# A one-pass score product for the row maximum, and the exact scores turned by keys, in the attention of a two-layer encoder trunk

## The chip, the cores and the metric

The kernel runs on one core of a Trainium2 chip. The metric is the device time of one execution in microseconds (us). A core has a matrix engine (PE, TensorE, with its weight loads shown apart as PEld), a vector engine (DVE), an activation engine (ACT), a general engine (POOL, GpSimd) and a queue engine (SP) that here only issues transfers. Each works through its own instructions in the order in which they stand; an instruction waits until the ones it depends on, on other engines, are done, and whatever stands behind it on the same engine waits with it.

## The reference, cut to what matters

Two layers work on 512 tokens of width 1024. A layer has a first gated feed-forward step, a mixing step and a second feed-forward step, with norms between. The mixing step has two groups side by side: attention with 8 heads, and a causal convolution over the tokens with 31 taps on 512 channels, followed by a layer norm over the channels and a swish. Both are put side by side and go through one output product.

```
scores = einsum('bhqd,bhkd->bhqk', qs, ks) * scale          # per block of 128 queries, keys up to the block's end
scores = where(k_chunk <= q_chunk, scores, -1e30)           # chunks of 64 tokens
probs  = softmax(scores)
out    = einsum('bhqk,bhkd->bqhd', probs, vs)
...
y = conv(u, conv_w) + conv_b                                # 31 taps, each channel for itself
conv = silu(layer_norm(y))
x = x + concat(attn, conv) @ w_out
```

So a head needs, for every query, the exponential of its scores less something near the largest of them, the sum of these, and the product with the values.

## The kernel before

All products of activations and weights run as three one-pass products of rounded parts (`mm3`, lines 151 to 154: high by high, high by low, low by high; the rounded type is called fp32r). Inside the attention the products are of the full four-byte type f32.

The mixing step of a layer is one function, `mix_body`. It makes the latents, queries and keys, then works through the heads in a software pipeline (lines 874 to 880): the string `ORDER` (line 58) gives each stage a lag in heads, so that step s works on head s in `turn`, head s-1 in `scores`, head s-3 in `turn_p`, and so on.

- `turn` (L804, L809) transposes a head's queries and keys on PE, 4 blocks each, so that the 100 rows (96 features and 4 rows that carry the chunk mask) lie on partitions. ACT writes the queries with their gain (L806), DVE the keys (L811).
- `scores` (L824) takes for each of the four blocks of 128 queries the product with the 128, 256, 384 or 512 keys that it may see; DVE finds the negated maximum of each row (L825), ACT takes the exponential with it as bias (L829). Queries lie on partitions.
- `turn_p` (L843) transposes the 10 blocks of probabilities on PE, and DVE, ACT and DVE copy them back (L846).
- `values` (L854) takes the 10 products of turned probabilities with 65 columns, 64 of values and one of ones, which gives the sum; DVE divides (L860, L861).
- `turn_out` (L871) transposes each pair of heads, and the result is cut into a high and a low part.

The convolution stands behind the heads in the program but has other operands. `CONV = "DAAD"` (line 42) says who does it: chunks 0 and 3 on DVE (L894), chunks 1 and 2 by ACT, which scales a shifted copy (L898, into one of three buffers called `pr`), and POOL, which adds it up (L902), 30 taps to a chunk. I call "tap n" the addition with n columns; the second chunk on POOL (the tile y_2856 in layer 0, y_2859 after the change) runs from tap 511 down to tap 482. POOL then adds the four chunks (L916 to L918), and PE takes the mean over channels with a matrix of 1/512 (L920, into `pm`). Behind L920 stand, on PE, the first half of the output product for three groups (`early_groups`, L909 to L912, which needs only the attention), then the rest of the layer norm and of the output product.

What sets the order: the program is given to a scheduler that plays it through with its own durations and fixes the order of the instructions on each engine. What it fixed is not changed while the kernel runs. Two lines hold it: the taps from the sixteenth of chunk 1 on, and all of chunk 2, must stand behind the last rsqrt of the keys (L901), and the early groups behind the last head's exponential (L909).

Of the kernel before, what the change touches and what calls it, by code (L numbers as in the profile page):

```python
# [15 lines left out]
P = 128  # L16
D = 1024
S = 512
# [6 lines left out]
DQ = DN + DR  # L25
DM = DQ + 4
DV = 64
# [18 lines left out]
POOLW = "wo"  # L46
QFOLD = 0
EARLY = "s"
# [7 lines left out]
WOP = 4  # L56
EVP = "DAD"
ORDER = "t0s1p3v4o5"

# [13 lines left out]
def encoder_kernel(ctx: ExitStack, tc: tile.TileContext, xT, consts, vecs, rgain, wgu1, wd1,  # L73
# [23 lines left out]
    def bank():  # L97
        return psum.tile([P, S], FP, tag="ps", name=nm("ps"))
# [26 lines left out]
    V.memset(onesm, 1.0 / CW)  # L125
    marks = cpool.tile([P, 2, NT, NT], FP, name="marks")
    G.memset(marks, 0.0)
    for t in range(NT):
        G.memset(marks[0:64, 0, t, t:t + 1], 1.0)
        G.memset(marks[64:P, 1, t, t:t + 1], -1e30)  # L130
# [478 lines left out]
    def mix_body(kpool, l, gx, norm, done):  # L609
# [3 lines left out]
        def glu(pa, pg):  # L613
# [7 lines left out]
            u.append(uc)  # L621

        def conv_in(c):
            pp = []
            for j in range(2):
                ps = bank()
                group(ps, load_w(wcv[l, 2 * c + j], WC, f"c{c}"), gx, range(KD), KD)
                pp.append(ps)
            glu(*pp)

# [11 lines left out]
        for side, v in enumerate((q, kn)):  # L642
            G.tensor_copy(v[:, :, :, DQ:DM], marks[:, side, :, None, :].to_broadcast([P, NT, H, NT]))
        cq, wkl_, sk, ckc, ratio = (tiny(n, NT) for n in ("cq", "wkl", "sk", "ckc", "ratio"))
# [80 lines left out]
        def queries():  # L725
            wq = [load_w(wuq[l, :, k * 768:(k + 1) * 768], 768, "uq") for k in range(3)]
            for t in range(NT):
# [17 lines left out]
                if t % 2:  # L745
                    rope(q[:, t - 1:t + 1, :, DN:DQ], tabs[0][:, :, t - 1:t + 1], H)
                    if not QFOLD:
                        for i in (t - 1, t):
                            V.tensor_tensor(q[:, i, :, 0:DQ], q[:, i, :, 0:DQ], scqs[i][:, :, None].to_broadcast([P, H, DQ]),
                                            ALU.mult)  # L750

# [49 lines left out]
        def turn(h):  # L801
            ps = bank()
            for t in range(NT):
                T.transpose(ps[0:DM, t * P:(t + 1) * P], q[:, t, h], ident)  # L804
            qT = slot()
            A.activation(qT[0:DM], ps[0:DM], AF.Copy, scale=gqs[0:DM])  # L806
            ps = bank()
            for t in range(NT):
                T.transpose(ps[0:DM, t * P:(t + 1) * P], kn[:, t, h], ident)  # L809
            kT = slot()  # L810
            V.tensor_scalar(kT[0:DM], ps[0:DM], gk, None, ALU.mult)  # L811
            heads[h]["qk"] = qT, kT

        def scores(h):
            qT, kT = heads[h]["qk"]
            b01, b2, b3 = bank(), bank(), bank()
            mx = small.tile([P, NT], FP, tag="mx", name=nm("mx"), bufs=3)
            pi = []
            ps = [slot() for _ in range(3)]
            ps = [ps[0][:, 0:128], ps[0][:, 128:384], ps[1][:, 0:384], ps[2]]  # L820
            for i in range(NT):
                n = (i + 1) * P
                o = (b01[:, 0:128], b01[:, 128:384], b2[:, 0:384], b3)[i]
                heads[h]["s"] = T.matmul(o, qT[0:DM, i * P:(i + 1) * P], kT[0:DM, 0:n], start=True, stop=True).ins  # L824
                V.tensor_reduce(mx[:, i:i + 1], o, axis=AX.X, op=ALU.max, negate=True)  # L825
                p = ps[i]
                if QFOLD:
                    V.tensor_tensor(mx[:, i:i + 1], mx[:, i:i + 1], scqs[i][:, h:h + 1], ALU.mult)
                A.activation(p, o, AF.Exp, bias=mx[:, i:i + 1], scale=scqs[i][:, h:h + 1] if QFOLD else 1.0)  # L829
                pi.append(p)  # L830
            heads[h]["p"] = pi

        def turn_p(h):

            pi = heads[h]["p"]
            pt = []
            for js, eng in (((0,), EVP[0]), ((1, 3), EVP[1]), ((2,), EVP[2])):
                ps = bank()
                sb = slot()
                o = 0  # L840
                for j in js:
                    for i in range(j, NT):
                        heads[h]["t"] = T.transpose(ps[:, o:o + P], pi[i][:, j * P:(j + 1) * P], ident).ins  # L843
                        o += P
                    pt.append((j, sb[:, o - (NT - j) * P:o]))
                (A.copy if eng == "A" else V.tensor_copy)(sb[:, 0:o], ps[:, 0:o])  # L846
            heads[h]["pt"] = [p for _, p in sorted(pt, key=lambda e: e[0])]

# [24 lines left out]

        STAGES = [({"t": turn, "s": scores, "p": turn_p, "v": values, "o": turn_out}[c], int(d)) for c, d in zip(ORDER[::2], ORDER[1::2])]
# [287 lines left out]
```

## Time and profile before

| | us |
|---|---|
| median of 3 runs | 1766.07 (1764.32 to 1767.33) |
| the profiled execution's own time | 1766.88 |
| its span, first to last instruction | 1765.1 |
| PE busy | 1745.7 (99%) |
| DVE, ACT, POOL busy | 1400.8, 942.5, 271.4 |
| start of the heads' scores on PE, layer 0 and 1 | 448.37, 1321.84 |
| start of L920, layer 0 and 1 | 503.06, 1376.49 |

The page gives a busy time per engine over the whole span; the stage that the change is in is about 70 us of each layer. There the timeline (start, duration, engine, line, shape, count, and in brackets the idle time before with what ended it) and the windows (busy time of each engine in a stretch, with counts) are what is to be read. A row of the timeline merges neighbours: "x26" is 26 instructions, and its duration runs from the start of the first to the end of the last. An f32 product with 128 to 512 columns makes two records on PE, a transpose makes one. Durations of single PE products overlap their neighbours, so what a product costs is read from start to start.

### The profile page before, as it was taken

The numbers are of one execution on the slowest core, as the hardware profiler recorded it, in microseconds if no ns is written. First come the engines' busy times: TensorE is split into PE (matmuls) and PEld (weight loads), VectorE is DVE, ScalarE is ACT, GpSimd is POOL, SyncE is SP. The second block draws the span as 40 slices with busy tenths as digits, with TensorE's granted clock in tenths as the row PEclk, the third lists the DMA queues.
The fourth block names the chain that finished last, engine by engine and source line by source line (L and its number), as shares of the span: only waits on it lengthen the run. The fifth ranks groups of instructions, "written<-read, shape, count | busy, mean of one in ns | idle before, by whom it ended". The sixth has DMA issues, their size and how long they took to land.

```text
span 1765.1 us, 22117 instructions
## 1 busy us (share of the span) xinstructions
PE 1745.7 (99%) x8102; PEld 1448.1 (82%) x8102; DVE 1400.8 (79%) x2033; ACT 942.5 (53%) x1420; POOL 271.4 (15%) x234
## 2 busy tenths in 40 slices
PE   9999999999999999999999999999999999999998
PEld 7888888888788888888888888888887888888886
DVE  8967878679869877869799778866889698678884
ACT  7544445457955544445555344444679455344453
POOL 2000000048942000000000000000579400000000
PEclk9999999999999999999999999999999999999999
DMA  9354434424225355352924445343251444544345
GB/s 294 129 179 138 139 119 122 141 76 123 60 108 132 129 158 167 96 167 83 293 89 142 145 132 167 95 144 107 79 137 31 147 106 136 174 143 145 106 134 153
DMA packets 121917, 236.70 MB, mean 134 GB/s; under 512 B 10705, under 2 KB 58321, under 8 KB 121809
## 3 DMA queue, kind: packets, MB, share of 16 engines
q1 hardware_dynamic: 117488, 222.08, 39.3%
q0 software_dynamic: 3456, 12.58, 3.9%
q8 instruction: 63, 1.03, 0.2%
q10 hardware_dynamic: 864, 0.64, 0.1%
q14 instruction: 46, 0.37, 0.1%
HBM read 207.99 MB, written 25.17 MB: 132 GB/s over the span
## 4 chain that ended last, share of the span: by engine, by line
PE 83%; DMA 6%; DVE 4%; ACT 2%; POOL 2%; issue 2%; SPq 1%; POOLq 0%; ACTq 0%; DVEq 0%
PE ps L154 26%; PE ps L152 26%; PE ps L153 26%; PE ps L854 2%; DMA fr<-in_wgu 2%; POOL y L902 1%; DVE wl L239 1%; DMA raw<-in_wgu 1%; PE ps L824 1%; DMA d<-e 1%; DMA r<-d 1%; PE ps L843 1%; ACT pr L898 1%; DVE fr L336 0%; ACT r L829 0%
## 5 line engine op out<-in xcount | busy, mean ns | idle before, releaser
L153 PE MATMUL ps<-wl,r 128*128 128x512 f32 (+2 forms) x1434 | 548.5, 384 | 1.4 <-DVE wl L239 1.4
L154 PE MATMUL ps<-wh,r 128*128 128x512 f32 (+2 forms) x1434 | 545.6, 384 | 0.2 <-DVE r L265 0.2
L152 PE MATMUL ps<-wh,r 128*128 128x512 f32 (+2 forms) x1434 | 530.2, 385 | 2.2 <-ACT wh L237 1.7
L237 ACT CAST wh<-fr 128x1024 fp32r<-128x1024 f32 x255 | 267.1, 1049 | 237.6 <-PE ps L153 108.6
L154 PE MATMUL ps<-r,wl 128*128 128x512 f32 x944 | 366.3, 390 | 0.7 <-POOL wl L147 0.5
L153 PE MATMUL ps<-r,wh 128*128 128x512 f32 x944 | 366.2, 390 | 0.0
L152 PE MATMUL ps<-r,wh 128*128 128x512 f32 x944 | 362.4, 393 | 1.1 <-ACT r L394 0.3
L239 DVE TENSOR_TENSOR wl<-fr,wh 128x1024 fp32r<-128x1024 f32 x255 | 310.1, 1219 | 52.0 <-ACT wh L237 51.0
L152 PEld LDWEIGHTS ps<-wh,r 128*128 128x128 f32 x1434 | 270.1, 189 | 55.2 <-ACT wh L237 2.6
L153 PEld LDWEIGHTS ps<-wl,r 128*128 128x128 f32 x1434 | 269.9, 188 | 53.9 <-DVE wl L239 1.9
L154 PEld LDWEIGHTS ps<-wh,r 128*128 128x128 f32 x1434 | 269.8, 188 | 52.4 <-DVE r L265 0.6
L141 ACT CAST wh<-raw 128x1024 fp32r<-128x1024 f32 (+2 forms) x142 | 139.7, 989 | 216.4 <-PE ps L153 96.5
L152 PEld LDWEIGHTS ps<-r,wh 128*128 128x128 f32 x944 | 177.1, 188 | 41.2 <-ACT r L394 1.7
L154 PEld LDWEIGHTS ps<-r,wl 128*128 128x128 f32 x944 | 177.2, 188 | 38.9 <-POOL wl L147 1.3
L153 PEld LDWEIGHTS ps<-r,wh 128*128 128x128 f32 x944 | 177.3, 188 | 38.4 <-issue 1.4
L147 DVE TENSOR_TENSOR wl<-raw,wh 128x1024 fp32r<-128x1024 f32 (+3 forms) x126 | 145.9, 1159 | 76.4 <-ACT wh L141 75.6
L902 POOL TENSOR_TENSOR y<-y,pr 128x511 f32<-128x511 f32 (+14 forms) x120 | 158.4, 1320 | 51.1 <-ACT pr L898 43.6
L336 DVE TENSOR_TENSOR fr<-fr,fr 128x1024 f32<-128x1024 f32 x112 | 136.6, 1220 | 12.6 <-DMA fr<-in_wgu 12.6
L484 DVE TENSOR_TENSOR x<-ps,x 128x512 f32<-128x512 f32 x120 | 81.5, 686 | 54.4 <-PE ps L154 54.1
L366 ACT ACTIVATE e<-e,rtok 128x256 f32<-128x256 f32 x120 | 59.9, 507 | 79.1 <-DVE e L357 78.4
L898 ACT ACTIVATE pr<-r,vec 128x511 f32<-128x511 f32 (+14 forms) x120 | 85.0, 734 | 13.7 <-POOL y L902 13.7
L395 DVE TENSOR_TENSOR r<-r,r 128x512 fp32r<-128x512 f32 x88 | 58.0, 681 | 41.5 <-ACT r L394 41.4
(197 smaller groups left out, 1668.2 us busy)
## 6 DMA issues: line engine op xcount, KB each, us to landing
fr<-in_wgu SPq DMA_DIRECT2D x175, 512.0 KB, 4.2
raw<-in_wd SPq DMA_DIRECT2D x56, 512.0 KB, 4.3
d<-e SPq DMA_DIRECT2D x176, 128.0 KB, 3.1
r<-d SPq DMA_DIRECT2D x88, 256.0 KB, 3.2
raw<-in_wd SPq DMA_DIRECT2D x32, 384.0 KB, 3.9
raw<-in_wcv SPq DMA_DIRECT2D x16, 512.0 KB, 3.3
raw<-in_wout SPq DMA_DIRECT2D x16, 512.0 KB, 4.1
raw<-in_wgu SPq DMA_DIRECT2D x8, 512.0 KB, 8.8
```

The lines of the kernel that those rows point to most:

```text
L141: A.copy(hi[:, :w], raw[:, :w])
L147: (G if kind in POOLW.split() else V).tensor_tensor(lo[:, :w], raw[:, :w], hi[:, :w].bitcast(FP), ALU.subtract)
L152: T.matmul(o, lh, rh, start=first, stop=False, skip_group_check=free)
L153: T.matmul(o, lh, rl, start=False, stop=False, skip_group_check=free)
L154: T.matmul(o, ll, rh, start=False, stop=last, skip_group_check=free)
L237: order["cast"] = A.copy(hi[:, :w], src[:, :w]).ins
L239: V.tensor_tensor(lo[:, :w], src[:, :w], hi[:, :w].bitcast(FP), ALU.subtract)
L336: V.tensor_tensor(oh, ah, bh, ALU.add)
L366: A.activation(out[j][:, :h], src[j][:, :h], AF.Silu, scale=r)
L484: V.tensor_tensor(xm, pd.rearrange("p (a t j) -> p t a j", a=4, t=NT), xm, ALU.add)
L898: A.activation(pr[:, s:], u[c][:, :S - s], AF.Copy, scale=tap(k))
L902: order["conv"] = G.tensor_tensor(acc[:, s:], acc[:, s:], pr[:, s:], ALU.add).ins
```

## The change

Each head's queries and keys get one row more (`DM` is 101): 1 in the keys, and in the queries a place, `MAXROW`, which is filled later. `turn` writes both sides on ACT (`TURN = "AA"`), and POOL makes a copy of each in the one-pass type fp32r (`r`, L815 of the changed kernel), 101 partitions by 512. A new stage `maxima` takes the scores of these copies in one pass, and DVE their row maxima, negated, as before; DVE then transposes the 128x128 tile that holds them, and SP sends the four rows of 128 into `MAXROW` of the exact queries in four transfers. Two heads later, `scores` takes the exact products the other way round: the keys are the stationary side, so keys lie on partitions and queries along the row, and since the 101st row adds the negated maximum, ACT needs no bias. The exponential gives turned probabilities at once; `turn_p` and its copies are gone. The two products of conv chunk 3, which stood together in step 1, now stand around `maxima`.

```diff
-DM = DQ + 4
+DM = DQ + 5
+MAXROW = DM - 1
-EVP = "DAD"
-ORDER = "t0s1p3v4o5"
+ORDER = "t0m1s3v4o5"
+TURN = "AA"
...
+    G.memset(marks[:, 1, :, NT:NT + 1], 1.0)
+    mx = cpool.tile([P, S // 4], FR, name="mx")
...
         def turn(h):
...
+            qk = []
+            for v, g, eng in ((q, gqs[0:DM], TURN[0]), (kn, gk, TURN[1])):
+                ps = bank()
+                for t in range(NT):
+                    T.transpose(ps[0:DM, t * P:(t + 1) * P], v[:, t, h], ident)
+                o = slot()
+                if eng == "A":
+                    A.activation(o[0:DM], ps[0:DM], AF.Copy, scale=g)
+                else:
+                    V.tensor_scalar(o[0:DM], ps[0:DM], g, None, ALU.mult)
+                r = slot(FR)
+                G.tensor_copy(r[0:DM], o[0:DM])
+                qk.append((o, r))
+            heads[h]["qk"], heads[h]["r"] = zip(*qk)
+
+        def maxima(h):
+
+            qT, kT = heads[h]["r"]
+            b01, b2, b3 = bank(), bank(), bank()
+            for i, o in enumerate((b01[:, 0:128], b01[:, 128:384], b2[:, 0:384], b3)):
+                T.matmul(o, qT[0:DM, i * P:(i + 1) * P], kT[0:DM, 0:(i + 1) * P], start=True, stop=True)
+                V.tensor_reduce(mx[:, i * 32:i * 32 + 1], o, axis=AX.X, op=ALU.max, negate=True)
+            mt = small.tile([P, S // 4], FP, tag="mt", name=nm("mt"))
+            V.transpose(mt, mx.bitcast(FP))
+            row = heads[h]["qk"][0][MAXROW:DM].rearrange("o (t g r) -> o t g r", t=NT, g=4)
             for t in range(NT):
...
+                nc.sync.dma_start(out=row[:, t], in_=mt[0:P:32, t * 32:(t + 1) * 32])
 
         def scores(h):
             qT, kT = heads[h]["qk"]
...
+            b0, b13, b2 = bank(), bank(), bank()
+            os = (b0, b13[:, 0:384], b2[:, 0:256], b13[:, 384:512])
+            for j in (0, 1, 3, 2):
+                T.matmul(os[j], kT[0:DM, j * P:(j + 1) * P], qT[0:DM, j * P:S], start=True, stop=True)
+            p0, p13, p2 = slot(), slot(), slot()
+            for p, o in ((p0, b0), (p13, b13), (p2[:, 0:256], b2[:, 0:256])):
+                heads[h]["s"] = A.activation(p, o, AF.Exp).ins
+            heads[h]["pt"] = [p0, p13[:, 0:384], p2[:, 0:256], p13[:, 384:512]]
...
                 if stage is turn and step == 1:
-                    conv_in(3)
+                    pa = conv_part(3, 0)
+                if stage is maxima and step == 1:
+                    glu(pa, conv_part(3, 1))
```

The scheduler places the new work as follows (layer 0; layer 1 has the same order in these places). First POOL, before, where the second chunk of the convolution begins (y_2855 is chunk 1, y_2856 chunk 2, `pr` the scaled copies):

```order
L902 TENSOR_TENSOR y_2855<-y_2855,pr_4468 128x483
L902 TENSOR_TENSOR y_2855<-y_2855,pr_4471 128x482
L902 TENSOR_TENSOR y_2856<-y_2856,pr_4475 128x511
L902 TENSOR_TENSOR y_2856<-y_2856,pr_4478 128x510
L902 TENSOR_TENSOR y_2856<-y_2856,pr_4481 128x509
L902 TENSOR_TENSOR y_2856<-y_2856,pr_4484 128x508
L902 TENSOR_TENSOR y_2856<-y_2856,pr_4487 128x507
```

and the same place of the changed kernel, where the casts of heads 5, 6 and 7 (queries, then keys) stand between the taps:

```order
L898 TENSOR_TENSOR y_2859<-y_2859,pr_4446 128x511
L815 CAST r_3963<-r_3961 101x512
L815 CAST r_3972<-r_3970 101x512
L898 TENSOR_TENSOR y_2858<-y_2858,pr_4442 128x482
L898 TENSOR_TENSOR y_2859<-y_2859,pr_4449 128x510
L815 CAST r_4025<-r_4023 101x512
L815 CAST r_4034<-r_4032 101x512
L898 TENSOR_TENSOR y_2859<-y_2859,pr_4452 128x509
L815 CAST r_4097<-r_4095 101x512
L898 TENSOR_TENSOR y_2859<-y_2859,pr_4455 128x508
L815 CAST r_4106<-r_4104 101x512
L898 TENSOR_TENSOR y_2859<-y_2859,pr_4458 128x507
```

The last cast, of head 7's keys, now stands right ahead of tap 507; the ten casts of heads 0 to 4 stand among the taps ahead of this piece, the first of them behind tap 494 of chunk 1.

On PE, before, the turn of the last head (L804, L809) stands behind the values of head 2 (L854) and the scores of head 5 (the first row is their last product):

```order
L824 MATMUL ps_4033<-r_3965,r_3958 128x256
L854 MATMUL ps_4071<-v_2859,r_4001 128x65
L854 MATMUL ps_4071<-v_2860,r_3994 128x65
L871 MATMUL ps_4086<-cst,t_3949 128x128 x4
L804 MATMUL ps_4095<-cst,q_2868 100x128 x4
L809 MATMUL ps_4102<-cst,kn_2869 100x128 x4
L824 MATMUL ps_4109<-r_4031,r_4024 128x128
```

In the changed kernel it stands behind the values of head 2 as well (L848), with the maxima of head 6 (L824) and the exact scores of head 4 (L837) behind it:

```order
L848 MATMUL ps_4066<-v_2863,r_3999 128x65
L865 MATMUL ps_4081<-cst,t_3952 128x128 x4
L808 MATMUL ps_4090<-cst,q_2871 101x128 x4
L808 MATMUL ps_4099<-cst,kn_2872 101x128 x4
L824 MATMUL ps_4108<-r_4034,r_4025 128x128
L824 MATMUL ps_4109<-r_4034,r_4025 128x384
L824 MATMUL ps_4110<-r_4034,r_4025 128x512
L837 MATMUL ps_4125<-r_3898,r_3907 128x512
```

Ahead of that turn the maxima of heads 0 to 5 and the scores of heads 0 to 3 stand where the scores of heads 0 to 5 and the turned probabilities of heads 0 to 3 stood.

At the end of the heads on PE (changed kernel) the mean over channels, L916, keeps its place:

```order
L848 MATMUL ps_4270<-v_2862,r_4242 128x65
L848 MATMUL ps_4270<-v_2863,r_4241 128x65
L865 MATMUL ps_4284<-cst,t_4257 128x128 x4
L916 MATMUL ps_4573<-t_4569,onesm 128x512
L155 MATMUL ps_4577<-r_4086,wh_4295 128x512
L156 MATMUL ps_4577<-r_4087,wh_4295 128x512
```

It is the only instruction here that needs POOL's sums, and the early groups of the output product (L155 on) stand behind it, as they stood behind L920.

More of the change, by code (lines that the diff above doesn't have):

```diff
@@ L46 @@
 POOLW = "wo"
-QFOLD = 0
 EARLY = "s"
@@ L125, in encoder_kernel @@
     V.memset(onesm, 1.0 / CW)
-    marks = cpool.tile([P, 2, NT, NT], FP, name="marks")
+    marks = cpool.tile([P, 2, NT, DM - DQ], FP, name="marks")
     G.memset(marks, 0.0)
+    G.memset(marks[:, 1, :, NT:NT + 1], 1.0)
+    mx = cpool.tile([P, S // 4], FR, name="mx")
+    G.memset(mx.bitcast(FP), 0.0)
     for t in range(NT):
@@ L621, in glu, with conv_part @@
             u.append(uc)
+        def conv_part(c, j):
+            ps = bank()
+            group(ps, load_w(wcv[l, 2 * c + j], WC, f"c{c}"), gx, range(KD), KD)
+            return ps
         def conv_in(c):
[L624 to L629, printed above, removed]
+            glu(*[conv_part(c, j) for j in range(2)])
         gql, gkl = vv(l, "gql"), vv(l, "gkl")
@@ L642, in mix_body @@
         for side, v in enumerate((q, kn)):
-            G.tensor_copy(v[:, :, :, DQ:DM], marks[:, side, :, None, :].to_broadcast([P, NT, H, NT]))
+            G.tensor_copy(v[:, :, :, DQ:DM], marks[:, side, :, None, :].to_broadcast([P, NT, H, DM - DQ]))
         cq, wkl_, sk, ckc, ratio = (tiny(n, NT) for n in ("cq", "wkl", "sk", "ckc", "ratio"))
@@ L746, in queries @@
                     rope(q[:, t - 1:t + 1, :, DN:DQ], tabs[0][:, :, t - 1:t + 1], H)
[L747 to L750, printed above, removed]
+                    for i in (t - 1, t):
+                        V.tensor_tensor(q[:, i, :, 0:DQ], q[:, i, :, 0:DQ], scqs[i][:, :, None].to_broadcast([P, H, DQ]),
+                                        ALU.mult)
         def keys():
@@ L801, in turn @@
         def turn(h):
-            ps = bank()
-            for t in range(NT):
[L804 to L812, printed above, removed]
+            qk = []
@@ L814, in scores @@
         def scores(h):
             qT, kT = heads[h]["qk"]
[L816 to L847, printed above, removed]
+            b0, b13, b2 = bank(), bank(), bank()
@@ L872, in turn_out @@
             at.append(split(ps))
-        STAGES = [({"t": turn, "s": scores, "p": turn_p, "v": values, "o": turn_out}[c], int(d)) for c, d in zip(ORDER[::2], ORDER[1::2])]
+        STAGES = [({"t": turn, "m": maxima, "s": scores, "v": values, "o": turn_out}[c], int(d)) for c, d in zip(ORDER[::2], ORDER[1::2])]
         for step in range(H + 6):
```

1 line of the change is left out of this document (added).

## The prediction

> **What bounds the kernel now.** I read the page first: the busy shares, the slices and the chain that ended last.
>
> ```profile
> PE 1745.7 (99%) x8102; PEld 1448.1 (82%) x8102; DVE 1400.8 (79%) x2033; ACT 942.5 (53%) x1420; POOL 271.4 (15%) x234
> POOL 2000000048942000000000000000579400000000
> PE 83%; DMA 6%; DVE 4%; ACT 2%; POOL 2%; issue 2%; SPq 1%; POOLq 0%; ACTq 0%; DVEq 0%
> ```
>
> By these shares PE sets the time, and an edit that takes matrix work away should pay. But the change sits in the two stretches of some 70 us where POOL's slices read 9, so I took the windows of the head loop (PE, PEld, DVE, ACT, POOL busy; layer 0, its start, its body and what follows; then clock and transfers):
>
> ```profile
> 448.00:462.00 14.00, 12.40 (x65) 8.26 (x63) 12.23 (x24) 13.66 (x26) 11.94 (x11) 1.00 0.58 121
> 462.00:503.00 41.00, 40.01 (x306) 35.66 (x306) 39.14 (x83) 33.95 (x65) 38.52 (x31) 1.00 0.00 1
> 503.00:517.00 14.00, 13.94 (x62) 10.58 (x60) 8.22 (x14) 6.31 (x11) 1.04 (x2) 1.00 0.01 1
> ```
>
> From 462 to 503 PE, DVE and POOL are all full. Which of them ends last is told by the timelines of POOL and PE:
>
> ```profile
> 443.21 2.58 POOL L902 TENSOR_TENSOR y<-y,pr 128x491 f32<-128x491 f32 x2 [0.42 <-ACT pr L898]
> ...
> 446.46 5.45 POOL L902 TENSOR_TENSOR y<-y,pr 128x489 f32<-128x489 f32 x4
> ...
> 455.48 1.21 POOL L902 TENSOR_TENSOR y<-y,pr 128x483 f32<-128x483 f32 x1 [0.20 <-ACT pr L898]
> 457.60 1.22 POOL L902 TENSOR_TENSOR y<-y,pr 128x482 f32<-128x482 f32 x1 [0.91 <-ACT pr L898]
> 459.30 5.32 POOL L902 TENSOR_TENSOR y<-y,pr 128x511 f32<-128x511 f32 x4 [0.48 <-ACT pr L898]
> 464.90 34.19 POOL L902 TENSOR_TENSOR y<-y,pr 128x507 f32<-128x507 f32 x26 [0.28 <-ACT pr L898]
> 499.05 1.27 POOL L916 TENSOR_TENSOR t<-r,y 128x512 f32<-128x512 f32 x1
> ...
> 501.74 1.26 POOL L918 TENSOR_TENSOR t<-t,r 128x512 f32<-128x512 f32 x1
> ```
>
> ```profile
> 448.37 1.89 PE L824 MATMUL ps<-r,r 100*128 100x128 f32 x6
> ...
> 480.09 0.60 PE L804 MATMUL ps<-cst,q 128*100 128x128 f32 x4
> ...
> 480.96 1.89 PE L824 MATMUL ps<-r,r 100*128 100x128 f32 x6
> 482.69 1.26 PE L843 MATMUL ps<-cst,r 128*128 128x128 f32 x10
> 483.79 2.34 PE L854 MATMUL ps<-v,r 128*128 128x65 f32 x20
> 485.97 2.38 PE L824 MATMUL ps<-r,r 100*128 100x256 f32 x8
> 488.18 1.26 PE L843 MATMUL ps<-cst,r 128*128 128x128 f32 x10
> ...
> 502.50 0.63 PE L871 MATMUL ps<-cst,t 128*128 128x128 f32 x4 [0.83 <-DVE t L861]
> 503.06 1.13 PE L920 MATMUL ps<-t,onesm 128*128 128x512 f32 x2
> ```
>
> Two chains arrive together. POOL's third sum ends at 503.00; PE has finished its last head and starts L920, which takes that sum, at 503.06. From tap 507 at 464.90 POOL has 26 taps and 3 sums without a gap. The head loop is therefore held by PE and POOL at once, with no measurable slack on either, and the 99% of the page does not show it.
>
> **The change, part by part.** *PE* loses ten transposes a head: from L843 at 482.69 to the next start at 483.79, 1.10 us. The exact scores stream the same 1280 columns in four passes, turned round, so they stay at 2.21 us (485.97 to 488.18). What is added is the one-pass product. Its price by columns, from starts in the same stage:
>
> ```profile
> 424.75 0.39 PE L152 MATMUL ps<-r,wh 128*128 128x512 f32 x1
> 424.98 0.39 PE L153 MATMUL ps<-r,wh 128*128 128x512 f32 x1
> ...
> 407.42 0.33 PE L154 MATMUL ps<-wh,r 128*128 128x384 f32 x1
> 407.59 0.33 PE L152 MATMUL ps<-wh,r 128*128 128x384 f32 x1
> ```
>
> 512 columns cost 0.23, 384 cost 0.17, so 256 and 128 come to about 0.12 and 0.06: 0.58 a head. No row shows the one-pass type with 128 columns; at the four-pass rate (2.21/1280 a column) that product would be 0.22, and the sum 0.74. I take 0.58, since both rows lie on the one-pass line. PE thus has 0.36 to 0.52 us less per head, 6 to 8 us over 16 heads, if nothing else holds it.
>
> *DVE* loses a scaled copy and two copies out of PSUM and gains one 128x128 transpose; *ACT* gains the scaled copy of the keys and loses one copy and the bias form of four exponentials in three:
>
> ```profile
> L811 DVE TENSOR_SCALAR r<-ps,vec 100x512 f32<-100x512 f32 x8 | 5.9, 745 | 0.2 <-PE ps L809 0.2
> L846 DVE COPY r<-ps 128x512 f32<-128x512 f32 x8 | 5.5, 688 | 0.0
> L376 DVE STREAM_TRANSPOSE e<-e 128x256 f32<-128x256 f32 x120 | 52.3, 439 | 0.6
> L806 ACT ACTIVATE r<-ps,gqs 100x512 f32<-100x512 f32 x8 | 5.6, 704 | 0.0
> L846 ACT COPY r<-ps 128x512 f32<-128x512 f32 x8 | 4.9, 616 | 0.7 <-PE ps L843 0.7
> ```
>
> DVE has about 1 us a head less by its rows (0.75 + 0.69, less a transpose of at most 0.44), ACT at most 0.1 more. Neither ends the stage, so I put both at nothing: POOL's and PE's work covers them.
>
> *SP* gets four small transfers a head:
>
> ```profile
> d<-e SPq DMA_DIRECT2D x176, 128.0 KB, 3.1
> ```
>
> They stand behind the loads of the output weights and ahead of the next step's loads, which wait for the layer norm anyway, so nothing is late behind them. A row is needed two heads after its maxima, some 11 us of PE work; the nearest transfers of the page take 3.1 us from issue to landing. I put them at nothing; if that cover fails, PE waits in a stretch where, by the sum below, it has some 20 us to spare later.
>
> *POOL* gets 16 casts a layer, 101x512. The trace has no cast on POOL and one kind of copy:
>
> ```profile
> L643 POOL COPY q<-marks 128x128 f32<-128x128 f32 x2 | 0.6, 288 | 0.0
> L637 POOL MEMSET v<- 128x8 f32 x8 | 0.4, 113 | 556.0 <-DMA raw<-in_wd 556.0
> ```
>
> With 113 ns as the overhead the copy has 1.46 ns a column, so a cast is 0.113 + 512 x 1.46 ns = 0.86 us; without overhead it would be four times 288, 1.15; one input at the pace of DVE's L811 would be 0.60 to 0.75. I take 0.8 and keep 0.55 to 1.15. The Trainium skill (GPSIMD Engine Reference, section 4.1) says that one-input work on this engine runs at roughly line rate, against about half of that for two inputs; with its dispatch time that would be an estimated 0.58 us, and the sum below about 1796. No run here shows it.
>
> The sum now goes by one place. Tap 507, which started at 464.90, must now stand behind the cast of head 7's keys. Behind it the same 26 taps and 3 sums remain, so L916 starts 503.06 - 464.90 = 38.16 us after that cast ends. When does it end? Two things hold it.
>
> POOL's own queue: 16 casts of 0.8 are 12.8 us; the waits for `pr` that they can fill are 0.20 + 0.91 + 0.48 + 0.28 and one of 0.42, together 2.3. That alone ends at 464.90 + 10.5 = 475.4.
>
> Its input: the head is turned on PE, and PE took from 448.37 to 480.09 to come there. In that way lie six scores and four turned probabilities, 6 x 2.21 + 4 x 1.10 = 17.7 us; now four scores and six maxima, 4 x 2.21 + 6 x 0.58 = 12.3, that is 5.4 less. But PE now waits for casts at the start: head 2's keys are the sixth cast, behind tap 488, which ended near 449.2 (446.46 and two taps of 1.36), so it ends at 449.2 + 4.8 = 454.0, where PE comes at about 450.7 (448.37, two turns of 0.87, one maxima). That is 3.3 us against the 1.6 that PE stood idle from 448 to 462. The turn of head 7 so starts at 480.09 - 5.4 + 1.7 = 476.4. ACT copies the queries (0.7, done near 477.8), POOL casts them (478.6), does tap 508 (479.9), and casts the keys (480.7).
>
> The later one counts: 480.7 + 38.2 = 518.9, where L920 stood at 503.06: **15.8 us later a layer**. With casts of 0.55 PE waits less and the end is near 478.5 (13.6 later); with 1.15 PE waits more and it is near 484.5 (19.6 later). PE's gain is lost: it ends its last head before 500 and then stands for some 18 us, because L916 is next in its order and the early groups are behind it. After L916 the same work follows, and PE was full there (13.94 of 14.00), so the delay goes to the end whole. Layer 1 has the same two rows, 38.1 us apart:
>
> ```profile
> 1338.37 34.16 POOL L902 TENSOR_TENSOR y<-y,pr 128x507 f32<-128x507 f32 x26 [0.26 <-ACT pr L898]
> ...
> 1376.49 1.13 PE L920 MATMUL ps<-t,onesm 128*128 128x512 f32 x2
> ```
>
> One thing more follows from so long a stand. PE's first products after the start of the program are slow:
>
> ```profile
> 1.06 3.78 PE L119 MATMUL ps<-ones 128*128 128x128 f32 x16 [1.06 <-DVE ones L113]
> 5.32 1.69 PE L152 MATMUL ps<-wh,r 128*128 128x512 f32 x4 [0.48 <-ACT wh L404]
> ```
>
> ```profile
> PE ps L152 <- ACT wh L237: 1.7, 1, 1.7
> ```
>
> Sixteen records of 128 columns in four passes should be 8 x 0.22 = 1.8 us and took 3.78; four of 512 took 1.69, where three starts of 0.23 and a last product of 0.39 make 1.08. A cold start costs 2.0 + 0.6 = 2.6 us. Before, PE never waited longer than 1.7 us at a stretch (the last row, the longest of its waits: total, times, longest); I take 1 us a layer, from 0 (no row shows it in the middle of a run) to 2.6. The Trainium skill (TensorE: Matmul & The Clock Gate, "Why this matters for your kernels") warns of the same: a gap over about 3 us between bursts puts the array back to half rate; its window of 3.4 us at half rate would be an estimated 1.7 us a layer, and the trace's start agrees in kind, with 2.6.
>
> The sum: 1766.88 + 2 x (15.8 + 1.0) = 1800.5 for the execution profiled; it lay 0.8 above the median, so **1800**.
>
> **The rivals.** *Casts dearer, so that POOL paces the heads as well.* With 1.15 a cast and a cold start of 2.6 it is 2 x (19.6 + 2.6) = 44, 1810. For it: the copy's 288 ns without overhead. Against: the memset shows that there is overhead.
>
> *The one-pass product isn't one-pass here.* If 101 partitions by 128 columns ran at the four-pass rate throughout, maxima would cost 2.21, head 7 would come 6 x 1.63 = 9.8 us later, and the time would be about 1820. Against: the 512 and 384 rows.
>
> *PE alone sets the pace, and the time falls.* The transposes are gone for less than they cost: 16 x 0.52 = 8 us, 1758. This needs the third sum on POOL to end no later than PE's last head, that is casts plus waits of less than 2.3 us a layer, 0.14 a cast, and taps that don't wait behind head 7. For it: PE at 99%, 83% of the chain. Against: POOL's 0.06 us of slack at L920, and the memset of 8 columns at 0.113. From a cast of about 0.14 us on it is decided the other way.
>
> *Gain and delay cancel* (within 0.2%, about what a measurement of this kernel tells from no change, 3.5 us): a delay of under 2 us a layer, which would need head 7's cast to end by 467, 9 us ahead of the time at which PE turns that head. No row supports it.
>
> **How the numbers follow.** The forecast with casts from 0.55 to 1.0 has 0.70, and its own range is 2 x (13.6 + 0) to 2 x (18 + 2), 1793 to 1806. Dearer casts have 0.15, the slow product 0.04, a smaller delay than mine (ACT or POOL finding slack in an order that I walked through by hand, 1775 to 1793) 0.06, the fall 0.03, no change 0.02. The range for 8 in 10 goes from 1786 to 1813. Faster by over 0.2%: 0.03; within: 0.02; slower: 0.95.
>
> **What would show it.** In the changed profile: L916 on PE with an idle time of 15 to 20 us before it, ended by POOL L914, in both layers; the last cast ending near 481 and 38 us from there to L916; casts of 0.8 us; maxima of 0.6 us a head by starts; slow products just behind L916. I am wrong if PE reaches L916 without a wait, if casts take under 0.3 us, or if the time lies below 1786 with POOL still last.

## The result and the profile after

The changed kernel takes 1809.52 us (median of 4 runs, 1808.22 to 1813.84), the kernel before on the same chip 1766.47 (4 runs). The ratio is 1.025, with a 95% interval of 1.0229 to 1.027. The execution profiled took 1808.44, with a span of 1806.6.

From the page of the changed kernel, the busy shares, POOL's and PE's clock slices, and the chain that ended last:

```profile
PE 1746.0 (97%) x8006; PEld 1446.8 (80%) x8006; DVE 1382.6 (77%) x2001; ACT 942.3 (52%) x1404; POOL 289.7 (16%) x268
POOL 2000000057752000000000000000687420000000
PEclk9999999999979999999999999999999799999999
PE 81%; POOL 6%; DVE 5%; issue 3%; ACT 2%; DMA 2%; SPq 0%; POOLq 0%; ACTq 0%; DVEq 0%
```

PE has fewer records and no less busy time; POOL's part of the chain has gone from 2% to 6%, and in each layer there is a slice in which PE's clock was lowered. PE's waits over the whole run (total, times, longest) say where:

```profile
PE ps L916 <- POOL t L914: 35.9, 2, 18.0
PE ps L824 <- POOL r L815: 7.8, 2, 3.9
PE ps L155 <- ACT wh L240: 1.7, 1, 1.7
```

PE now stands 18 us in each layer at the mean over channels, for POOL's third sum, and 3.9 us inside the heads for a cast. POOL's timeline of layer 0 shows how the sum came to be late:

```profile
454.81 1.90 POOL L815 CAST r<-r 101x512 fp32r<-101x512 f32 x3
...
475.48 1.19 POOL L815 CAST r<-r 101x512 fp32r<-101x512 f32 x2 [2.29 <-ACT r L811]
...
481.83 0.61 POOL L815 CAST r<-r 101x512 fp32r<-101x512 f32 x1 [3.92 <-ACT r L811]
482.40 1.27 POOL L898 TENSOR_TENSOR y<-y,pr 128x508 f32<-128x508 f32 x1
483.61 0.61 POOL L815 CAST r<-r 101x512 fp32r<-101x512 f32 x1
484.18 5.27 POOL L898 TENSOR_TENSOR y<-y,pr 128x507 f32<-128x507 f32 x4
490.22 10.61 POOL L898 TENSOR_TENSOR y<-y,pr 128x503 f32<-128x503 f32 x8 [0.76 <-ACT pr L894]
...
521.49 1.26 POOL L914 TENSOR_TENSOR t<-t,r 128x512 f32<-128x512 f32 x1
```

Tap 507 starts at 484.18, right behind the cast of head 7's keys; before, it started at 464.90. In front of the casts POOL stands idle, up to 3.92 us; taps 508 and 507, behind them, had their scaled copies from ACT since 478. PE's timeline of the same layer:

```profile
455.57 1.33 PE L824 MATMUL ps<-r,r 101*128 101x128 f32 x3 [3.91 <-POOL r L815]
456.70 4.47 PE L837 MATMUL ps<-r,r 101*128 101x512 f32 x8
...
469.01 0.76 PE L824 MATMUL ps<-r,r 101*128 101x128 f32 x3
469.61 2.32 PE L837 MATMUL ps<-r,r 101*128 101x512 f32 x8
473.02 0.36 PE L824 MATMUL ps<-r,r 101*128 101x256 f32 x1
473.22 1.00 PE L848 MATMUL ps<-v,r 128*128 128x65 f32 x8
...
480.39 0.60 PE L808 MATMUL ps<-cst,q 128*101 128x128 f32 x4
...
522.81 2.07 PE L916 MATMUL ps<-t,onesm 128*128 128x512 f32 x2 [17.98 <-POOL t L914]
531.10 0.95 PE L193 MATMUL ps<-ones,acc 128*128 128x1 f32 x8
```

The same eight records of exact scores take 4.47 us behind the wait of 3.91 and 2.32 elsewhere. The windows (PE, PEld, DVE, ACT, POOL busy, then the granted clock, that is the share of PE's full clock that the profile records, as a mean over the window) show the same thing from the clock's side:

```profile
456.00:463.00 7.00, 7.00 (x24) 5.00 (x24) 6.79 (x12) 3.65 (x8) 4.53 (x6) 0.58 0.20 39
...
523.00:527.00 4.00, 4.00 (x9) 2.49 (x10) 2.08 (x4) 1.36 (x3) 0.00 (x0) 0.54 0.00 0
527.00:535.00 8.00, 8.00 (x40) 6.71 (x39) 3.24 (x6) 1.07 (x2) 1.04 (x1) 1.00 0.00 0
```

To see where the 41.5 us of span went, I cut each profiled execution at three places per layer: the first turn of a head on PE, the start of the mean (L916; L920 before), and the start of the first product of the norm behind it (L193; L190 before). All are differences of starts on PE's timeline, layer 0 and layer 1:

| kernel | turn to mean | mean to norm | all the rest | span |
|---|---|---|---|---|
| before | 67.43, 67.38 | 6.45, 6.46 | 1617.4 | 1765.1 |
| after | 87.85, 87.87 | 8.29, 8.53 | 1614.1 | 1806.6 |

The stretch from the first turn to the mean grew by 20.4 and 20.5 us, the restart behind it by 1.8 and 2.1. Together that is 44.8; 3.3 came back in the rest of the program, which in the fourteen profiles of this study lies between 1613.9 and 1619.9 us. From the first turn to the mean POOL was busy 61.9 us of 67.4 before and is busy 70.6 of 87.9 now: 8.7 us more work and 11.7 us more idle time.

### The profile page after: what moved, and what is told of

Same layout as the page of the kernel before. It is cut to its first block, busy times and chain, and to the rows that moved or that the text cites. A ratio compares the mean times of both kernels' runs of the same rounds, so it can differ in the third digit from the quotient of the medians.

```text
span 1806.6 us, 22073 instructions
## 1 busy us (share of the span) xinstructions
PE 1746.0 (97%) x8006; PEld 1446.8 (80%) x8006; DVE 1382.6 (77%) x2001; ACT 942.3 (52%) x1404; POOL 289.7 (16%) x268
## 4 chain that ended last, share of the span: by engine, by line
PE 81%; POOL 6%; DVE 5%; issue 3%; ACT 2%; DMA 2%; SPq 0%; POOLq 0%; ACTq 0%; DVEq 0%
PE ps L155 26%; PE ps L157 26%; PE ps L156 26%; POOL y L898 4%; DVE cv L890 1%; DVE wl L242 1%; PE ps L837 1%; PE ps L848 1%; DMA raw<-in_wgu 1%; DVE fr L339 1%; ACT pr L894 1%; PE ps L193 0%; DMA rg<-in_rgain 0%; DMA x<-in_xT 0%; PE ps L824 0%
## 5 line engine op out<-in xcount | busy, mean ns | idle before, releaser
L155 PE MATMUL ps<-wh,r 128*128 128x512 f32 (+2 forms) x1434 | 529.3, 384 | 2.7 <-ACT wh L240 1.7
L155 PE MATMUL ps<-r,wh 128*128 128x512 f32 x944 | 364.0, 395 | 0.7 <-ACT wh L144 0.5
L155 PEld LDWEIGHTS ps<-wh,r 128*128 128x128 f32 x1434 | 269.4, 188 | 55.1 <-ACT wh L240 2.6
L155 PEld LDWEIGHTS ps<-r,wh 128*128 128x128 f32 x944 | 177.8, 189 | 40.6 <-ACT r L161 1.1
L898 POOL TENSOR_TENSOR y<-y,pr 128x509 f32<-128x509 f32 (+15 forms) x120 | 158.2, 1319 | 48.8 <-ACT pr L894 42.7
L890 DVE SCALAR_TENSOR_TENSOR cv<-r,vec,cv 128x511 f32<-128x511 f32 (+14 forms) x120 | 88.0, 733 | 5.9 <-ACT cv L886 3.8
```

Of the source, the lines that this page charges most:

```text
L155: T.matmul(o, lh, rh, start=first, stop=False, skip_group_check=free)
L890: V.scalar_tensor_tensor(acc[:, s:], u[c][:, :S - s], tap(k), acc[:, s:], ALU.mult, ALU.add)
L898: order["conv"] = G.tensor_tensor(acc[:, s:], acc[:, s:], pr[:, s:], ALU.add).ins
```

## The experiments

Each run's ratio is to the kernel before, timed beside it on the same chip.

### The casts alone, and all the rest without them

First run: the changed kernel with the rounded copies written by DVE from PSUM; POOL does none.

```diff
-                G.tensor_copy(r[0:DM], o[0:DM])
+                V.tensor_scalar(r[0:DM], ps[0:DM], g, None, ALU.mult)
```

> The changed kernel with the rounded copies written by DVE out of PSUM instead of by POOL (32 casts fewer on POOL, 32 DVE writes of about 0.65 us more); nothing else differs. Theory (the 16 casts a layer and their place among POOL's taps hold the mean over channels): the 18.0 us wait ahead of L916 and the 3.9 us wait of the maxima for a cast go, POOL again ends its sums near 503, and the time is 1762 to 1772. Rival (the new stage itself, with its row transfers, its waits and PE's slow restarts, costs the time on PE): PE still reaches the end of its heads late and the time stays above 1785.

Second run: the kernel before, with the sixteen casts added on POOL. Nothing reads them.

```diff
+            for o in (qT, kT):
+                r = slot(FR)
+                G.tensor_copy(r[0:DM], o[0:DM])
```

> The kernel before, with 16 casts a layer on POOL that nobody reads; PE's work and waits are those of before. In POOL's order 31 taps and 3 sums stand behind the cast of head 7's keys. If the casts act by their place (a tap can't start before head 7's keys are written, 483 on the trace of before, plus a cast of 0.6, plus 34 x 1.29 = 44 us), L920 comes at about 527, 24 us late a layer, and the time is 1812 to 1822 with the slow restart. If they act by their load alone (16 x 0.6 less the 2.3 us of waits they can fill, 7 us a layer), it is 1779 to 1786. If POOL isn't what holds the end, it is 1766.

The first takes 1768.24 us, 1.0015 (1.0006 to 1.0024); the second 1820.82, 1.0313 (1.0296 to 1.033). So the casts on POOL are the loss, nearly whole: without them the change costs 2.5 us, and they alone cost the old kernel 55. POOL in the second run:

```profile
479.70 0.61 POOL L815 CAST r<-r 100x512 fp32r<-100x512 f32 x1 [2.36 <-ACT r L806]
480.27 1.22 POOL L905 TENSOR_TENSOR y<-y,pr 128x483 f32<-128x483 f32 x1
481.43 0.62 POOL L815 CAST r<-r 100x512 fp32r<-100x512 f32 x1
482.00 2.44 POOL L905 TENSOR_TENSOR y<-y,pr 128x511 f32<-128x511 f32 x2
```

Here the scheduler put the last cast ahead of tap 511, four taps further up than in the changed kernel, so L923 (the mean) waits 27.55 us and stands 25.6 us later after the first turn than before (93.06 for 67.43). The casts are 16 x 0.57 = 9.1 us of work; they cost 25.6 by where they stand. The load reading (1779 to 1786) is out.

In the first run POOL is done at 501.7 and L916 starts at 504.21 without a wait for it. What holds PE there is the same place in the heads, now for DVE's copy:

```profile
PE ps L824 <- DVE r L815: 9.3, 4, 4.5
```

### Is PE's idle time the loss, or what stands behind the mean?

The early groups of the output product need no sum. Third run: all three ahead of the mean on PE.

```diff
-E1 = 0
+E1 = 3
-E2 = 2
+E2 = 3
```

> The changed kernel with the three early groups of the output product (36 products, 8.2 us) placed ahead of the mean over channels on PE instead of behind it. The wait ahead of L916 falls from 18.0 to about 10 us on either theory. If the chain behind L916 (mean, squares, rsqrt, spread, swish: 15.9 us from L916 to the first product that needs it) sets the end, this filling buys only the part of that chain that was PE's own work, 0 to 2.5 us a layer: 1804 to 1810. If the end is set by the sum of PE's work and PE was merely idle, it gains the 8 us twice: 1793.

It takes 1811.33 us, 1.0259 (1.0244 to 1.0274): no gain, a microsecond above the range of the first reading, 1804 to 1810. The waits of that run, over both layers:

```profile
PE ps L916 <- POOL t L914: 19.9, 2, 10.0
PE ps L193 <- DVE acc L188: 9.7, 2, 4.9
...
PE ps L211 <- DVE t L207: 4.4, 2, 2.2
```

PE fills 8 us of its 18, and then has nothing to do while DVE works through the layer norm that starts with the mean. The stand is moved behind L916, not removed: it is POOL, mean, norm that set the end.

### Less work on POOL

Fourth run: the first 12 additions of the second POOL chunk on DVE.

```diff
-                if kind == "D":
+                if kind == "D" or c == 2 and s <= 12:
```

> The changed kernel with the first 12 taps of conv chunk 2 on DVE (fused, 0.65 us each) instead of ACT and POOL: POOL does 12 x 1.27 = 15.2 us less a layer behind the last cast, and the casts stay where they are. If POOL's taps behind the last cast set L916, its wait falls from 18.0 to about 3 us and the time is 1809.5 - 2 x (15 + 1 to 2) = 1775 to 1780. If PE or DVE were the bound, the 8 us more on DVE would show instead, and the time would be 1805 or more.

It takes 1793.53 us, 1.0161 (1.0146 to 1.0176): 16 us less than the changed kernel where I expected 30 to 35. The wait at L916 is nearly gone (2.1 us in one layer, none in the other), but the place is taken by DVE:

```profile
PE ps L824 <- DVE mx L825: 14.3, 4, 4.2
PE ps L824 <- POOL r L815: 3.7, 4, 1.4
PE ps L837 <- DVE mx L825: 3.6, 2, 2.0
```

The row maxima stand on DVE behind additions that were put there early, so the heads come later: head 7's turn stands 54.5 us after the first turn in layer 0, for 45.4. PE was slower as well: its granted clock from the first turn to the mean was 0.89 in both layers, where the kernel before had 1.00. DVE had no room either.

### The wait inside the heads

PE's wait of 3.91 us for a cast was no part of my sum at this size. Fifth run: the second product of conv chunk 3, some 5.5 us of PE work, one step later, so that it stands ahead of that wait.

```diff
-                if stage is maxima and step == 1:
+                if stage is maxima and step == 2:
```

> Edit to the changed kernel: the second product of conv chunk 3 stands behind the maxima of head 1 (step 2) and no longer behind those of head 0 (step 1), so PE has some 5.5 us of work between the turn of head 2 and the maxima of head 2, where it waited 3.91 us for GpSimd's cast and then ran at a granted clock of 0.58. Theory (that wait and the slow products behind it moved head 7's turn by 3.9 + 2.9 us, and with it the last cast and L916): the wait in front of the maxima falls below 1 us, the windows of the head loop show a clock of 1.00, head 7's turn starts 4 to 6.8 us earlier, L916 as well, and the time is 1796 to 1803. Rival (the wait in the head loop costs nothing, since POOL's own load of casts and taps fixes L916): L916 stays within 1.5 us and the time is 1807 to 1811.

It takes 1810.17 us, 1.0245 (1.0231 to 1.0259); the forecast of 1796 to 1803 failed. Waits of layer 0's heads, PE's timeline at the maxima of heads 2 and 3, and the windows (granted clock third from the end):

```profile
PE ps L837 <- DVE mx L825: 1.9, 1, 1.9
PE ps L824 <- POOL r L815: 1.9, 1, 1.9
```

```profile
455.69 0.77 PE L824 MATMUL ps<-r,r 101*128 101x128 f32 x3
...
461.74 1.24 PE L824 MATMUL ps<-r,r 101*128 101x128 f32 x3 [1.88 <-POOL r L815]
```

```profile
461.50:464.00 2.50, 2.26 (x5) 1.52 (x6) 2.39 (x4) 2.50 (x7) 1.89 (x3) 0.57 0.62 117
...
472.00:475.00 3.00, 3.00 (x4) 1.36 (x5) 3.00 (x9) 0.60 (x1) 1.61 (x2) 0.52 0.00 0
```

The wait at head 2's maxima is gone, as intended. But waits of 1.9 us now stand at head 3's maxima, for a cast, and ahead of exact scores, for DVE's maxima, with slow products behind both; a third, of 1.6 us, stands ahead of the moved product, for ACT's copy. Head 7's turn came 1.6 us later after the first turn than in the changed kernel (47.07 for 45.43), and 4.5 later in layer 1, not earlier. L916 came 3.8 us earlier in layer 0 and 1.0 in layer 1, since four taps now stood ahead of the last cast; the medians do not show these 4.8 us. In the profiled execution as much was lost outside the stretch from the first turn to the norm, where all the rest took 1618.6 us for 1614.1. So the wait for the cast was not the only thing that kept PE back at that spot, and the edit cannot price it.

### The slow products behind the stand

Sixth run: 80 products of 128x128 that nothing reads, on PE in front of L916.

```diff
+        with tc.issue_after(order["at"]):
+            idle(80)
```

> Edit to the changed kernel: 80 products of 128x128 that nothing reads are put on PE between the last head's transposes (L865) and L916, some 17 us of work in the stand of 18.0 us. Nothing else changes. Theory (the products behind L916 are slow because PE stood): the granted clock behind L916 is 1.00, L916 to L193 takes 6.5 us as in the kernel before and not 8.3, and the time falls by 2 x 1.8 us to 1805 to 1807. Rival (the products behind L916 are slow for another reason, operands that come late or the bandwidth of the load of weights): 1809 to 1812.

Here the mean is L918. Its timeline and a window:

```profile
524.56 1.12 PE L918 MATMUL ps<-t,onesm 128*128 128x512 f32 x2 [0.21 <-POOL t L916]
531.00 0.95 PE L193 MATMUL ps<-ones,acc 128*128 128x1 f32 x8
```

```profile
523.00:527.00 4.00, 3.79 (x22) 2.85 (x21) 1.28 (x3) 0.76 (x2) 1.43 (x2) 1.00 0.00 0
```

The clock is 1.00 and the mean is 6.44 us ahead of the norm (6.31 in layer 1), for 8.29 and 8.53 after and 6.45 before. The stand does make the products behind it slow, at about 2 us a layer. The time, though, is 1811.14, 1.0244 (1.0228 to 1.026), not lower. In the profiled execution the 4.1 us are lost elsewhere: the first turn of layer 0 stands 1.65 us later than in the changed kernel, with the same instructions on PE ahead of it, the stretch between the layers took 3.4 us more, and layer 1's heads 1.5. That first turn stands between 434.43 and 437.47 in the fourteen profiles of this study, and four runs of one kernel spread by up to 5.6 us; an effect of 4 us cannot be told from four runs here. It is shown in its place and not in the time.

### How far a cast may stand from the end

Seventh and eighth run: the casts of head 7 alone, then of heads 6 and 7 (`h >= 6`), on DVE.

```diff
-                G.tensor_copy(r[0:DM], o[0:DM])
+                (V if h >= 7 else G).tensor_copy(r[0:DM], o[0:DM])
```

> Edit to the changed kernel: the two casts of head 7 alone are done by DVE, the other 14 of a layer stay on POOL. Place theory (tap 507 and all behind it stand behind the last cast that POOL has to wait for): the last cast is now head 6's, which ended at 476.64; behind it come taps 509 and 508 (2 x 1.27 us) and the same 38.6 us, so L916 starts near 517.8, 5.0 us earlier a layer, and the time is 1797 to 1802. Load theory (each cast costs L916 its own 0.58 us): 1.2 us earlier a layer, 1806 to 1808.

> The same with the four casts of heads 6 and 7 on DVE. Place theory: the last cast is head 5's, which ended at 470.77; behind it come four taps (4 x 1.24 us) and the 38.6 us, so L916 starts near 514.3, 8.5 us earlier a layer, and the time is 1790 to 1796, if ACT's copies keep the pace. Load theory: 2.3 us a layer, 1804 to 1806.

They take 1806.50 us, 1.0232 (1.0219 to 1.0245), and 1800.24, 1.0197 (1.0184 to 1.0211): the first in the load range, the second in neither. From the first turn L916 comes 2.2 us earlier a layer (85.63) and 4.8 (83.07): about twice the load reading (1.2 and 2.3), and half the place reading (5.0 and 8.5). With head 7's casts gone from POOL, its taps meet this (timeline of POOL, then of ACT, in the seventh run):

```profile
476.06 3.94 POOL L898 TENSOR_TENSOR y<-y,pr 128x509 f32<-128x509 f32 x3
482.51 1.26 POOL L898 TENSOR_TENSOR y<-y,pr 128x506 f32<-128x506 f32 x1 [2.51 <-ACT pr L894]
484.68 16.02 POOL L898 TENSOR_TENSOR y<-y,pr 128x505 f32<-128x505 f32 x12 [0.91 <-ACT pr L894]
```

```profile
480.50 0.69 ACT L811 ACTIVATE r<-ps,gqs 101x512 f32<-101x512 f32 x1
481.08 0.69 ACT L811 ACTIVATE r<-ps,vec 101x512 f32<-101x512 f32 x1
481.65 0.72 ACT L894 ACTIVATE pr<-r,vec 128x506 f32<-128x506 f32 x1
```

The scaled copy that tap 506 adds stands on ACT behind ACT's own copies of head 7 (the two L811), which wait for PE's turn of head 7. So the convolution was tied to head 7 twice, by POOL's order and by ACT's; taking away the first leaves the second.

### A version that beats the kernel before?

Four more kernels try. All write the rounded keys from PSUM on DVE and have the later product of conv chunk 3; `step` and the casts are the edits shown above.

The first has all casts on DVE:

> The run with casts on DVE (1768.2) and the later second product of conv chunk 3 together. There PE still waited 4.3 us for DVE's copy at the maxima of head 2, while POOL had its third sum done 2.5 us ahead of L916. Theory (with that wait gone PE's heads end some 5 us earlier, and POOL's sum at 501.7 becomes the last): L916 starts at 501 to 502.5 with a wait of 2 to 4 us ended by POOL, and the time is 1763 to 1766. Rival (DVE with its 20 more us of copies is what holds the heads): PE still reaches L916 at 504 or later without a wait for POOL, 1767 to 1771.

It takes 1766.29 us against 1766.54, 0.9998 (0.9989 to 1.0007): the same as before. From turn to mean it takes 67.42 and 67.40 us, the old figures, and PE and POOL arrive together again: POOL's third sum ends at 501.98, L916 starts at 502.03. So the mean came where the theory put it, without the wait of 2 to 4 us that it expected. In layer 1 PE did wait, 1.3 us:

```profile
1375.86 1.27 PE L916 MATMUL ps<-t,onesm 128*128 128x512 f32 x2 [1.30 <-POOL t L914]
...
1383.91 0.95 PE L193 MATMUL ps<-ones,acc 128*128 128x1 f32 x8
```

From the mean to the norm it took 8.05 us there, for 6.46 before: even this short wait has slow products behind it.

The second adds three taps on DVE (`c == 2 and s <= 3`):

> The run with casts on DVE and the later product of conv chunk 3, and beside these the first 3 taps of conv chunk 2 on DVE and not on POOL, so that POOL's third sum ends 4 us earlier, near 498. Theory (PE and POOL are then close together again, PE with its 0.3 us a head less): 1757 to 1764, ahead of the kernel before. Rival (3 taps of 0.6 us on DVE make the row maxima late, as 12 taps did): 1766 to 1772.

It takes 1773.53 us, 1.0032 (1.0019 to 1.0044): the rival's direction, a little beyond its range. DVE's copies come later still (8.5 us of PE's waits over both layers), POOL's third sum waits 3.27 us for the copy of conv chunk 3, whose additions DVE does, and the clock falls to 0.54 where waits of 0.4 to 1.1 us stand close together.

The third gives the rounded queries to ACT:

```diff
+                if v is q:
+                    A.activation(r[0:DM], ps[0:DM], AF.Copy, scale=g)
+                else:
+                    V.tensor_scalar(r[0:DM], ps[0:DM], g, None, ALU.mult)
```

> Edit to the run with all casts on DVE and the later second product of conv chunk 3 (1766.3): the rounded queries are written by ACT from PSUM, the rounded keys by DVE. There PE waited 2.6 us a layer for DVE's copies, and L916 started at 502.0 and 1375.9. Theory (DVE holds the heads): with 6 us less on DVE a layer these waits fall below 1 us, PE's last head ends near 500, POOL's sum at 500 to 502 becomes the last, and the time is 1761 to 1766. Rival (ACT is full too, 19.8 of 21 us in the middle of the heads, so its scaled copies for POOL's taps come late): POOL's third sum ends at 504 to 508, 1768 to 1778.

It takes 1777.12 us, 1.007 (1.0054 to 1.0085). POOL's chunk now starts late, for want of ACT's copies:

```profile
461.84 1.28 POOL L901 TENSOR_TENSOR y<-y,pr 128x511 f32<-128x511 f32 x1 [1.04 <-ACT pr L897]
465.49 23.92 POOL L901 TENSOR_TENSOR y<-y,pr 128x510 f32<-128x510 f32 x18 [2.37 <-ACT pr L897]
```

POOL's third sum ends at 508.8, and PE is later still: its waits for DVE's copies rose to 7.6 us over both layers from 5.3, and the mean starts at 512.21. DVE's own load was not what held the heads: ahead of its copy for head 3, at 460.48, DVE stood idle 1.95 us for a copy of ACT's. The 2.3 us of added waits do not explain that the mean came 9.3 and 8.4 us later than without the edit. The granted clock goes with it: from the first turn to the mean it was 0.89 and 0.86, for 1.00 and 1.00. The missing shares of 76.7 and 75.8 us make an estimated 8.4 and 10.6 us of lost clock. The profiled execution, at 1781.83, lay 4.7 us above the median. How much ACT's load cost by itself, no run here separates. The last keeps this edit and moves the third sum to DVE (`YP = 0`):

> The same with the third sum of the four chunks on DVE and not on POOL (1.26 us there). Theory (POOL's sum is what L916 waits for): L916 1 to 1.3 us earlier a layer than in the run without this edit, 1759 to 1764 if that one is at 1761 to 1766. Rival (PE or ACT's copies set L916): within 1 us of that run.

It takes 1777.24 us, 1.0075 (1.0063 to 1.0087), within 1 us of the run before it. No version here beats the kernel before. With the casts on POOL, on DVE, and on DVE with ACT, PE or POOL came to wait for the engine that took them. And where the waits in the heads lay close together the clock fell with them: from the first turn to the mean it was 1.00 in the first of these four, 0.95 and 0.93, 0.89 and 0.86, 0.87 and 0.91 in the others, with no single wait there above 2.2 us.

## Why the prediction was right, point by point

It said 1800, with 1786 to 1813; the time is 1809.5. The mechanism is the one forecast; three of its terms were too small, one was too large, and one was missing.

- **Two chains with no slack, POOL's the one that loses.** Shown by the first two experiments: the casts taken from POOL bring back all but 2.5 us, the casts alone added to the old kernel cost 55.
- **Tap 507 behind head 7's keys, and 38.16 us from there to the mean.** The last cast ends by 484.18 and the mean starts at 522.81: 38.63. It held.
- **Casts of 0.8 us.** Too dear. By starts they are 0.57 (483.61 to the tap at 484.18), and three in a row took 1.90. The estimate from the Trainium skill (GPSIMD Engine Reference, section 4.1) was 0.58, and the trace agrees with it. That the time came out above the forecast and not at the 1796 of that sentence lies with the next points.
- **Maxima of 0.58 us a head.** The mis-sized term: 469.01 to 469.61 for three products and 473.02 to 473.22 for the fourth make 0.80, so PE's gain is 0.30 a head and not 0.52. By the single starts in this trace the products of 128, 256, 384 and 512 columns took 0.14, 0.20, 0.22 and 0.23, where I had 0.06, 0.12, 0.17 and 0.23: the line through the rows of 384 and 512 columns, which stood among other one-pass products, does not hold here. Six heads' maxima ahead of head 7's turn make 1.3 us.
- **A wait of 3.3 us for head 2's cast.** It was 3.9 us. What the sum left out is what such a wait does to the products behind it: the scores took 4.47 us for 2.32 and the maxima 1.33 for 0.76, another 2.7 us. This is the missing term: I had counted a cold restart behind the long stand and none inside the heads.
- **Head 7's turn at 476.4.** It stood at 480.39; counted from the first turn, 45.4 us for the 40.8 that I had, 4.7 later. The three sizes just named make 1.3 + 0.6 + 2.7 = 4.6. That it closes so well is in part luck: a wait of 0.55 us for DVE's maxima (at 464.48) and some 0.3 us of slow turns and maxima behind the slow scores stand outside it. With head 7's turn 4.7 us later, 15.8 us a layer becomes the 20.4 that the table shows.
- **A cold restart of 1 us behind the stand.** It was 1.8 and 2.1, and it is the stand that causes it (the run with the added products). The estimate from the Trainium skill (TensorE: Matmul & The Clock Gate, "Why this matters for your kernels") was 1.7; the trace agrees.
- **DVE, ACT and SP at nothing.** SP held: PE waited for no row of maxima. DVE cost the 0.55 us just named and ACT nothing that shows, because POOL was later than both. They were no cover in reserve: with the casts on DVE, PE waited 4.5 us for DVE, and ACT's order held POOL's taps once head 7's casts were gone.

The sum with the measured terms is 20.4 + 20.5 + 1.8 + 2.1 = 44.8 us, less 3.3 in the rest of the program, which no step foresaw. No run explains these 3.3 us; they lie within the 6 us by which the rest differs between the profiles. Of the rivals, "casts dearer" gave the right size, 1810, for a wrong reason: the casts were cheaper than forecast and POOL waited for their input.

## What to carry to other kernels

On an engine that works in a fixed order, price an added instruction by when its input comes, not by how long it takes: here 9 us of casts cost 20 to 26, because 26 additions and more, which needed nothing from them, stood behind the last. Before giving work to an engine with a low busy share, look at its slices in that stage and at what is queued behind the new instruction; and when one such tie is cut, look for a second one in the engine that feeds it. Add to every new wait on the matrix engine the slow products that follow it.

## What the hardware showed that was not expected

**A short wait can be enough to lower the matrix engine's clock.** Behind a wait of 3.9 us the granted clock was 0.58 over 7 us, and waits of 1.9 us in the fifth run were followed by 0.57 and 0.52. In the variant with three taps on DVE, four waits of 0.4 to 1.1 us within 6 us were followed by 0.54 and then 0.50. In layer 0 of the run that equals the kernel before, waits of at most 1.3 us, with PE busy at least 5.7 of each 7 us, left it at 1.00. In its layer 1, waits of 0.8 and 1.3 us ahead of the mean, with 0.6 us of work between them, were followed by 0.59. Length alone does not decide: one wait of 1.8 us in the run with the added products (layer 1, at 1362) and one of 1.84 in the variant with three taps on DVE (layer 0, at 463.7) were followed by 1.00. What decides was not tested. The Trainium skill (TensorE: Matmul & The Clock Gate, "HAM oscillation — how this bites in real kernels") names gaps over some 3.4 us as what to avoid; here half of that could suffice, so the measurement decides.

**The slow start costs about the same behind a short wait and a long one.** From the mean to the norm the kernel before took 6.45 us. Behind waits of 1.3 and 2.1 us at the mean it took 8.05 and 8.01 (one layer each of the run with casts on DVE and the later product, and of the run with 12 taps on DVE), behind 11.7 us 8.00 to 9.19 (casts of heads 6 and 7 on DVE), behind 18 us 8.29 and 8.53 (the changed kernel), behind 27.5 us 8.02 and 8.26 (casts alone). A wait of 0.8 to 1.0 us for the last head's result stands just ahead in all of these, and in the kernel before.

**A small one-pass product has no price of its own.** With 101 partitions, one of 256 columns took 0.20 us from start to start ahead of full-type products (473.02 to 473.22 above) and 0.12 between other one-pass products (changed kernel):

```profile
447.49 0.28 PE L824 MATMUL ps<-r,r 101*128 101x256 f32 x1
447.61 0.40 PE L156 MATMUL ps<-r,wh 128*128 128x512 f32 x1
```

One of 512 columns took 0.23, and one of 128 behind a full-type transpose 0.14. What sets this was not tested. Among full-type products, turning a product into one pass pays by its columns only when it has many of them.
